# Two buffers of their own for the second token block's adding DMAs, and fourteen row block pairs at other places, in a two-layer decoder trunk

## The chip, the core and the metric

The kernel runs on one core of a Trainium2 chip. The metric is the time of one execution on the device in microseconds (us); where several executions are told, it is their median. A profiled execution gives a trace, and its span runs from the first to the last instruction of the program.

## The reference, cut to what matters

256 tokens of 2048 values pass two layers. Each layer has a token mixer (forgetting attention, then dilated attention) and an MLP, and everything is added into one residual stream `x`:

```
def sq_relu_mlp(h, w_up, w_down):
    a = jax.nn.relu(h @ w_up)          # 2048 -> 8192
    return (a * a) @ w_down            # 8192 -> 2048
...
for i in range(DEPTH):                 # 2 layers
    h = rms_norm(x, mix_norm_g[i])
    mix = fox_attention(...) if i % 2 == 0 else dilated_attention(...)
    x = x + mix
    h = rms_norm(x, mlp_norm_g[i])
    x = x + sq_relu_mlp(h, mlp_w_up[i], mlp_w_down[i])
```

All is float32. The change touches the two MLPs alone; in names, `n1` is the first layer's MLP and `n3` the second's.

## The kernel before

**Matrix products.** The tokens are two blocks of 128, `t=0` and `t=1`. A weight is loaded in raw row blocks of 256 rows by 512 columns (`raw`, five buffers, loaded from SyncE's queue, called SP). ACT copies such a block to a rounded high part (`wh`, line 370), DVE subtracts to get the low part (`wl`, line 371), five buffers each, and TensorE (PE) multiplies three times: high by high, high by low, low by high (lines 421 to 423). That is one *product unit*: 12 matmuls of 512 columns. By how much `wl` is done ahead of its use is called the lead here; ACT can run ahead of PE by the five buffers.

**The MLP.** Its 8192 hidden columns are four blocks, b = 0 to 3. For each block the up projection gives four chunks of 512 columns, which are squared and turned (lines 965 to 1013), and the down projection, `out_proj`, adds the block's part to `x` in four column chunks, n = 0 to 3. For blocks 1 to 3 the up projection's chunks 0 to 2 are computed in another way: a row block pair is cut in halves, and a 2 by 2 block product is done with seven products in place of eight (`SEVEN`, `slice_steps`). One such *pair* (the change's "row block pairs in halves") is one raw load, sums of weight quarters on DVE (`quarters`, lines 380 to 384), two casts and two subtractions (lines 366 to 371, shapes 128x768 and 128x1024), and 21 matmuls (lines 1056 to 1060, output `halves`). These pairs do not stand in a row: they are woven between the product units of the down projection of the block before. The tables `BETWEEN` and `FIRST_BETWEEN` (for b = 1) say after which product unit, counted from the start of that down projection, each of the 24 pairs of a block stands. Units 0 to 15 are chunks n = 0 and 1 in two parts, 16 to 23 are n = 2, 24 to 31 are n = 3, and 32 to 39 are the next block's up projection chunk 3.

**The adding DMAs.** For blocks 0 to 2 the sums of a down projection are not added by DVE but by DMA (`late` in `add_chain`): ACT scales half a chunk of one token block from PSUM into a buffer `y`, and a DMA from GpSimd's queue (POOL) adds it to `x`. A chunk has four y's, two for each token block. There are 4 chunks, 3 blocks and 2 MLPs, so 24 such places and 96 y's.

**What sets the order.** The code is one long program of generators that a counter of steps drives (`Jobs`, `tick`, one step per half product unit; `yield 4` waits four steps, and `clear(steps)` waits so that it wakes on the step without a cast). Each engine executes in exactly the order in which the program issued its instructions (`pin`). An instruction that waits therefore holds everything behind it on its engine. `split` issues the cast and subtraction of the unit five ahead, and issues the next raw load.

Of the kernel before, what the change touches and what calls it, by code (L numbers as in the profile page):

```python
# [9 lines left out]
F32 = mybir.dt.float32  # L10
# [7 lines left out]
P = 128  # L18
# [24 lines left out]
HC = NC // 2  # L43
# [2 lines left out]
SEVEN = ((0, 0, 2, 5), (1, 0, 0, 4), (2, 0, 1, 0), (3, 0, 7, 6), (0, 1, 5, 3), (1, 1, 6, 2), (2, 1, 4, 1))  # L46
SUM_TAGS = ("kh3", "kl3", "kh4", "kl4", "kh5", "kl5", "q0", "q1", "q2", "qkw0", "qkw1", "qkw2", "vh", "vl", "pT", "t1")

BETWEEN = (0, 1, 2, 3, 6, 7, 9, 11, 14, 15, 16, 17, 19, 20, 22, 23, 27, 28, 30, 32, 33, 34, 36, 37)
FIRST_BETWEEN = (0, 1, 2, 5, 7, 9, 10, 11, 15, 16, 17, 18, 20, 21, 22, 23, 27, 28, 30, 31, 33, 34, 36, 37)  # L50


class Jobs:
# [48 lines left out]
def trunk(ctx: ExitStack, tc, x, fox_w_in, fox_b_f, fox_q_gain, fox_k_gain, fox_w_out, dil_w_in,  # L102
# [5 lines left out]
    def clear(steps):  # L108

        return steps + (jobs.now + steps + 1) % 2  # L110
# [21 lines left out]
    work = ctx.enter_context(tc.tile_pool(name="work", bufs=1))  # L132
# [147 lines left out]
    def in_halves():  # L280

        for b in range(1, 4):
            for i, at in enumerate(BETWEEN if b > 1 else FIRST_BETWEEN):
                yield 40 * b - 8 + at, b, i // 8, i % 8
# [115 lines left out]
    def by_column(acc, apart=NC // 2):  # L400
        return acc.rearrange("p (b n h) -> p b h n", n=apart, h=2)

    def halves(t, apart=NC // 2):
        return t.rearrange("p (b h n) -> p b h n", n=apart, h=2)

    used = [0]
# [512 lines left out]
    def add_chain(acc, n, then, ready, scale, late):  # L919
        yield scale and (scale, "rstd") or 0  # L920
        for t in range(NT):
            at = halves(xt[n][:, t, :])
            if late:

                for h in range(2):
                    y = work.tile([P, HC], F32, tag="bias", name=f"y_{scale}_{n}_{t}_{h}_{used[0]}", bufs=2)
                    nc.scalar.activation(y, by_column(acc[t])[:, 0, h, :], AF.Copy, scale=rstd[scale, 2][:, t:t + 1])
                    nc.gpsimd.dma_start(xt[n][:, t, h * HC:h * HC + HC], y, accum_op=ALU.add)  # L928
                if t == 0:
                    yield clear(3)  # L930
                continue
            if scale:
                nc.vector.scalar_tensor_tensor(at, by_column(acc[t]), rstd[scale, 2][:, t:t + 1], at, ALU.mult, ALU.add)
            else:
                nc.vector.tensor_add(at, at, by_column(acc[t]))
            if ready is not None:
                ready(n, t)
        if then is not None:
            jobs.spawn(then(n))
        yield 0  # L940
# [10 lines left out]
    def out_proj(keys, lhs, then=None, ready=None, scale=None, group=0, parts=OUT_PARTS, late=False):  # L951
        posts = [lambda acc, n=n: add_chain(acc, n, then, ready, scale, late) for n in range(NX)]
        if group:
            in_group(lambda n: sums(*(() if n < 2 else (ps_sc, "sc") if scale else (ps_tp, "tp"))),
                     lambda acc, ks: product_steps(acc, keys, lhs, ks), posts[0:group], parts)
        for n in range(group, NX):
            if ready is not None and n == NX - 1:
                last_product(keys, lhs, final_add(n, scale))
            else:
                product(keys, lhs, posts[n])  # L960
# [200 lines left out]
    tag = "n0"  # L1161
# [56 lines left out]
```

## Time and profile before

| | |
|---|---|
| median of 3 runs | 2160.63 us (2159.32 to 2161.76) |
| the profiled execution's own time | 2162.61 us |
| its span | 2160.9 us |
| mean granted TensorE clock | 0.997 |
| PE busy | 2123.3 us (98%) |
| DVE busy | 1748.1 us (81%) |
| ACT busy | 1282.3 us (59%) |
| POOL busy | 138.9 us (6%) |

The first MLP's y's are written between 502.7 and 934.5 us, the second's between 1614.9 and 2050.1 us. An operand of matmul rows reads `out<-in`: `acc` is a product unit's PSUM sum, `halves` that of a pair. In a row of waits, the numbers are microseconds in total, how many times, and the longest. A matmul's duration overlaps the next one's, so pace is read from starts.

### The profile page before, as it was taken

Reading aid. Unit: us, or ns where it says so; the run is one execution under the profiler, and the core shown is the slowest. Engines: PE = TensorE matmul, PEld = TensorE weight load, DVE = VectorE, ACT = ScalarE, POOL = GpSimd, SP = SyncE. Lnnn points to the kernel's source line nnn. Section 1 sums busy time; section 2 is a strip of 40 time slices with the busy share of each in tenths; the row PEclk is TensorE's granted clock in tenths of the full one; section 3 lists DMA queues with packets and bytes.
Section 4 is the critical chain, followed back from the end, with each engine's and each line's share of the span. In section 5 each row is a group of like instructions: output and inputs, shape, how many; then the busy total and the mean of one; then the engine's idle time right before and its main releaser. Section 6 shows DMA issues by size and latency. Waiting matters only on the chain.

```text
span 2160.9 us, 32247 instructions
## 1 busy us (share of the span) xinstructions
PE 2123.3 (98%) x11375; PEld 1889.1 (87%) x11375; DVE 1748.1 (81%) x2548; ACT 1282.3 (59%) x1869; POOL 138.9 (6%) x160
## 2 busy tenths in 40 slices
PE   9999999999999999999999999999999999999999
PEld 7888888898888899898888888888898888888988
DVE  6888876798888898888668787767898798898874
ACT  6565655655665566565655565646655665665662
POOL 2000000001001100100010010000001101101100
PEclk9999999999999999999999999999999999999999
DMA  7888777877777777888877777868868777877784
GB/s 250 260 259 270 250 243 244 275 223 235 233 215 233 233 230 248 234 259 265 266 235 234 240 235 217 264 199 271 262 218 238 214 248 229 238 238 225 239 263 161
DMA packets 374993, 518.26 MB, mean 240 GB/s; under 512 B 43096, under 2 KB 176560, under 8 KB 374832
## 3 DMA queue, kind: packets, MB, share of 16 engines
q1 hardware_dynamic: 360592, 503.23, 73.3%
q0 software_dynamic: 13824, 12.59, 3.9%
q8 instruction: 89, 1.46, 0.3%
q14 instruction: 72, 0.59, 0.1%
q10 hardware_dynamic: 416, 0.39, 0.1%
HBM read 463.12 MB, written 40.39 MB: 233 GB/s over the span
## 4 chain that ended last, share of the span: by engine, by line
PE 64%; issue 12%; DVE 11%; DMA 6%; ACT 4%; POOL 1%; SPq 1%; ACTq 0%; DVEq 0%; POOLq 0%
PE acc L422 19%; PE acc L423 19%; PE acc L421 19%; DVE wl L371 5%; DMA x<-y_n 4%; ACT wh L370 3%; PE halves_n L1059 2%; PE halves_n L1060 2%; PE halves_n L1058 2%; DVE quarters L380 1%; POOL x L928 1%; DVE quarters L383 1%; DVE quarters L384 1%; DMA raw<-in_dil_w_in_dram 1%; DMA raw<-in_mlp_w_down_dram 1%
## 5 line engine op out<-in xcount | busy, mean ns | idle before, releaser
L371 DVE TENSOR_TENSOR wl<-raw,wh 128x1024 fp32r<-128x1024 f32 (+1 forms) x659 | 789.2, 1213 | 303.0 <-ACT wh L370 298.0
L370 ACT CAST wh<-raw 128x1024 fp32r<-128x1024 f32 (+1 forms) x659 | 677.4, 1043 | 402.5 <-PE acc L423 312.1
L421 PE MATMUL acc<-wh,hT_n 128*128 128x512 f32 x1344 | 513.0, 382 | 0.3 <-ACT hT_n L566 0.3
L422 PE MATMUL acc<-wl,hT_n 128*128 128x512 f32 x1344 | 509.7, 379 | 0.9 <-DVE wl L371 0.9
L423 PE MATMUL acc<-wh,hT_n 128*128 128x512 f32 x1344 | 509.5, 379 | 0.0
L370 ACT CAST wh<-quarters 128x1024 fp32r<-128x1024 f32 x144 | 150.7, 1046 | 267.4 <-DVE quarters L384 236.4
L423 PEld LDWEIGHTS acc<-wh,hT_n 128*128 128x128 f32 x1344 | 254.0, 189 | 36.2 <-DVE hT_n L567 0.2
L422 PEld LDWEIGHTS acc<-wl,hT_n 128*128 128x128 f32 x1344 | 254.4, 189 | 35.2 <-DVE wl L371 1.8
L421 PEld LDWEIGHTS acc<-wh,hT_n 128*128 128x128 f32 x1344 | 254.4, 189 | 34.5 <-ACT hT_n L566 0.6
L371 DVE TENSOR_TENSOR wl<-quarters,wh 128x1024 fp32r<-128x1024 f32 x144 | 175.9, 1222 | 50.4 <-ACT wh L370 50.4
L422 PE MATMUL acc<-wl,aTh_n1a 128*128 128x512 f32 x512 | 195.9, 383 | 3.4 <-DVE wl L371 3.1
L421 PE MATMUL acc<-wh,aTh_n1a 128*128 128x512 f32 x512 | 195.1, 381 | 2.9 <-ACT wh L370 2.8
L423 PE MATMUL acc<-wh,aTl_n1a 128*128 128x512 f32 x512 | 194.7, 380 | 0.0
L421 PE MATMUL acc<-wh,aTh_n3a 128*128 128x512 f32 x480 | 183.5, 382 | 4.1 <-ACT wh L370 3.9
L422 PE MATMUL acc<-wl,aTh_n3a 128*128 128x512 f32 x480 | 183.9, 383 | 3.3 <-DVE wl L371 3.1
L423 PE MATMUL acc<-wh,aTl_n3a 128*128 128x512 f32 x480 | 182.9, 381 | 0.0
L1060 PE MATMUL halves_n<-wh,sums_n 128*128 128x256 f32 x576 | 158.8, 276 | 0.0
L1059 PE MATMUL halves_n<-wl,sums_n 128*128 128x256 f32 x576 | 158.8, 276 | 0.0
L1058 PE MATMUL halves_n<-wh,sums_n 128*128 128x256 f32 x558 | 153.9, 276 | 0.0
L368 DVE TENSOR_TENSOR wl<-raw,wh 128x768 fp32r<-128x768 f32 x144 | 137.0, 952 | 2.0 <-ACT wh L366 2.0
L1059 PE MATMUL halves_n<-wl,hT_n 128*128 128x256 f32 x432 | 123.6, 286 | 12.9 <-DVE wl L371 10.8
L366 ACT CAST wh<-raw 128x768 fp32r<-128x768 f32 x144 | 119.7, 831 | 19.0 <-DMA raw<-in_mlp_w_up_dram 7.9
(664 smaller groups left out, 3381.4 us busy)
## 6 DMA issues: line engine op xcount, KB each, us to landing
raw<-in_mlp_w_up_dram SPq DMA_DIRECT2D x256, 512.0 KB, 4.8
raw<-in_mlp_w_down_dram SPq DMA_DIRECT2D x256, 512.0 KB, 4.8
raw<-in_dil_w_in_dram SPq DMA_DIRECT2D x192, 256.0 KB, 3.5
raw<-in_fox_w_in_dram SPq DMA_DIRECT2D x95, 512.0 KB, 4.9
raw<-in_fox_w_out_dram SPq DMA_DIRECT2D x32, 512.0 KB, 4.6
raw<-in_dil_w_in_dram SPq DMA_DIRECT2D x32, 512.0 KB, 4.6
raw<-in_dil_w_out_dram SPq DMA_DIRECT2D x32, 512.0 KB, 4.1
x<-y_n POOLq DMA_DIRECT2D x96, 128.0 KB, 5.0
```

The costliest lines, as they stand in the source:

```text
L366: nc.scalar.copy(flat_hi, flat)
L368: nc.vector.tensor_sub(flat_lo, flat, flat_hi.bitcast(F32))
L370: nc.scalar.copy(hi[:, part, :], raw[:, part, :])
L371: nc.vector.tensor_sub(lo[:, part, :], raw[:, part, :], hi[:, part, :].bitcast(F32))
L380: nc.vector.tensor_sub(t[:, 0, :].rearrange("p (q n) -> p q n", q=2), raw.rearrange("p k n -> p (k n)")[:, HC:3 * HC].rearrange("p (q n) - ...
L383: nc.vector.tensor_add(c, raw[:, 0, HC:NC], neg)
L421: nc.tensor.matmul(acc[t], ah[:, tok], hi, start=first, stop=False)
L422: nc.tensor.matmul(acc[t], ah[:, tok], lo, start=False, stop=False)
L423: nc.tensor.matmul(acc[t], al[:, tok], hi, start=False, stop=last)
L1058: nc.tensor.matmul(to, ah, hi, start=pr == 0 and i == 3, stop=False)
L1059: nc.tensor.matmul(to, ah, lo, start=False, stop=False)
L1060: nc.tensor.matmul(to, al, hi, start=False, stop=pr == KC // 2 - 1 and i > 2)
```

## The change

The y's of t=1 no longer share the two `bias` buffers with those of t=0. They take one buffer each under the tags `t0` and `t2`, which hold a mask and the distance tables of the attention stages and nothing in the MLPs. They are issued two steps earlier (`clear(1)` for `clear(3)`). In the tables, three of the 24 pairs of block 1 stand one product unit later; of blocks 2 and 3, one pair stands one unit later and one a unit earlier. With two MLPs that is 6 + 4 pairs later and 4 earlier.

```
-BETWEEN = (0, 1, 2, 3, 6, 7, 9, 11, 14, 15, 16, 17, 19, 20, 22, 23, 27, 28, 30, 32, 33, 34, 36, 37)
-FIRST_BETWEEN = (0, 1, 2, 5, 7, 9, 10, 11, 15, 16, 17, 18, 20, 21, 22, 23, 27, 28, 30, 31, 33, 34, 36, 37)
+BETWEEN = (0, 1, 2, 3, 6, 7, 9, 11, 14, 15, 16, 17, 19, 21, 22, 23, 27, 28, 30, 31, 33, 34, 36, 37)
+FIRST_BETWEEN = (0, 1, 2, 6, 8, 9, 10, 11, 15, 16, 17, 19, 20, 21, 22, 23, 27, 28, 30, 31, 33, 34, 36, 37)
...
                 for h in range(2):
-                    y = work.tile([P, HC], F32, tag="bias", name=f"y_{scale}_{n}_{t}_{h}_{used[0]}", bufs=2)
+                    of, bufs = ("bias", 2) if t == 0 else (("t0", "t2")[h], 1)
+                    y = work.tile([P, HC], F32, tag=of, name=f"y_{scale}_{n}_{t}_{h}_{used[0]}", bufs=bufs)
                     nc.scalar.activation(y, by_column(acc[t])[:, 0, h, :], AF.Copy, scale=rstd[scale, 2][:, t:t + 1])
                     nc.gpsimd.dma_start(xt[n][:, t, h * HC:h * HC + HC], y, accum_op=ALU.add)
                 if t == 0:
-                    yield clear(3)
+                    yield clear(1)
                 continue
```

The added line shifts the numbers of all later lines by one.

First place: ACT in the first MLP, at the end of column chunk 1 of the second block's down projection. Names are `y_n1_<chunk>_<t>_<half>_...`. Before:

```order
L366 CAST wh288_7145<-raw253_6986 128x768
L927 ACTIVATE y_n1_1_0_0_284_7153<-acc260_0_6665,rstd2_n1_4065 128x256
L927 ACTIVATE y_n1_1_0_1_284_7156<-acc260_0_6665,rstd2_n1_4065 128x256
L370 CAST wh289_7174<-quarters253_7148 128x1024
L370 CAST wh290_7189<-raw254_7038 128x1024
L927 ACTIVATE y_n1_1_1_0_286_7195<-acc260_1_6666,rstd2_n1_4065 128x256
L927 ACTIVATE y_n1_1_1_1_286_7198<-acc260_1_6666,rstd2_n1_4065 128x256
L370 CAST wh291_7213<-raw255_7065 128x1024
```

The same place on ACT after the change:

```order
L366 CAST wh288_7145<-raw253_6992 128x768
L928 ACTIVATE y_n1_1_0_0_284_7153<-acc260_0_6665,rstd2_n1_4065 128x256
L928 ACTIVATE y_n1_1_0_1_284_7156<-acc260_0_6665,rstd2_n1_4065 128x256
L928 ACTIVATE y_n1_1_1_0_284_7168<-acc260_1_6666,rstd2_n1_4065 128x256
L928 ACTIVATE y_n1_1_1_1_284_7171<-acc260_1_6666,rstd2_n1_4065 128x256
L370 CAST wh289_7180<-quarters253_7148 128x1024
L370 CAST wh290_7195<-raw254_7038 128x1024
L370 CAST wh291_7213<-raw255_7065 128x1024
```

The two y's of t=1 moved ahead of two casts, right behind those of t=0.

Second place: ACT in the first MLP, at the end of chunk 3 of the second block's down projection, where a pair moved from unit 32 to 31. Before:

```order
L366 CAST wh322_7820<-raw278_7716 128x768
L927 ACTIVATE y_n1_3_0_0_318_7828<-acc304_0_7532,rstd2_n1_4065 128x256
L927 ACTIVATE y_n1_3_0_1_318_7831<-acc304_0_7532,rstd2_n1_4065 128x256
L1008 CAST aTh_n1a2_0_7842<-turned_n1a2_0_0_7040 128x4x128
L1008 CAST aTh_n1a2_1_7845<-turned_n1a2_1_0_7607 128x4x128
L370 CAST wh323_7854<-quarters278_7823 128x1024
L370 CAST wh324_7871<-raw279_7735 128x1024
L1008 CAST aTh_n1a2_0_7842<-turned_n1a2_0_1_7091 128x4x128
L1008 CAST aTh_n1a2_1_7845<-turned_n1a2_1_1_7637 128x4x128
L927 ACTIVATE y_n1_3_1_0_320_7879<-acc304_1_7533,rstd2_n1_4065 128x256
L927 ACTIVATE y_n1_3_1_1_320_7882<-acc304_1_7533,rstd2_n1_4065 128x256
```

The same place on ACT after the change:

```order
L366 CAST wh322_7820<-raw278_7716 128x768
L370 CAST wh323_7837<-quarters278_7823 128x1024
L370 CAST wh324_7855<-raw279_7735 128x1024
L928 ACTIVATE y_n1_3_0_0_320_7861<-acc304_0_7532,rstd2_n1_4065 128x256
L928 ACTIVATE y_n1_3_0_1_320_7864<-acc304_0_7532,rstd2_n1_4065 128x256
L1009 CAST aTh_n1a2_0_7875<-turned_n1a2_0_0_7040 128x4x128
L1009 CAST aTh_n1a2_1_7878<-turned_n1a2_1_0_7607 128x4x128
L928 ACTIVATE y_n1_3_1_0_320_7881<-acc304_1_7533,rstd2_n1_4065 128x256
L928 ACTIVATE y_n1_3_1_1_320_7884<-acc304_1_7533,rstd2_n1_4065 128x256
```

The pair's matmuls now come before the y's of this chunk, so two casts stand ahead of the y's that stood behind them.

Third place: ACT in the first MLP, in block 1's first pairs (`FIRST_BETWEEN`, 5 to 6 and 7 to 8). Before:

```order
L370 CAST wh171_4763<-raw168_4632 128x1024
L366 CAST wh172_4778<-raw169_4659 128x768
L544 CAST sums_n1_6_0_4786<-room_n1_4076 128x512
L370 CAST wh173_4801<-quarters169_4781 128x1024
L370 CAST wh174_4820<-raw170_4709 128x1024
L1008 CAST aTh_n1a0_3_4834<-turned_n1a0_3_0_4635 128x4x128
```

The same place on ACT after the change:

```order
L370 CAST wh171_4763<-raw168_4632 128x1024
L370 CAST wh172_4778<-raw169_4659 128x1024
L544 CAST sums_n1_6_0_4784<-room_n1_4076 128x512
L366 CAST wh173_4799<-raw170_4709 128x768
L370 CAST wh174_4820<-quarters170_4802 128x1024
L1009 CAST aTh_n1a0_3_4834<-turned_n1a0_3_0_4635 128x4x128
```

The cast of a whole raw block (128x1024, from `raw`), which stood fifth, is now second, and the pair's two casts follow it.

## The prediction, as it was put on record

> **What bounds the kernel now.** I read the page first, then the waits of TensorE, then the tile `y_n` (the scaled sums that the adding DMAs take), then busy time by stage. The page says that TensorE is the bound, with little left over:
>
> ```profile
> span 2160.9 us, 32247 instructions
> PE 2123.3 (98%) x11375; PEld 1889.1 (87%) x11375; DVE 1748.1 (81%) x2548; ACT 1282.3 (59%) x1869; POOL 138.9 (6%) x160
> ```
>
> TensorE idles 2160.9 - 2123.3 = 37.6 us. From 500 to 2054 us, where both MLPs lie, it waits for the high and low weight parts that ACT (`wh`) and DVE (`wl`) make:
>
> ```profile
> PE halves_n L1059 <- DVE wl L371: 10.8, 21, 0.9
> PE acc L422 <- DVE wl L371: 6.8, 10, 0.8
> PE acc L421 <- ACT wh L370: 6.7, 5, 2.2
> PE halves_n L1058 <- ACT wh L370: 3.1, 2, 2.1
> ```
>
> The tile `y_n` tells what holds ACT. In its view the second part is what ACT, the writer, waited for ahead of these instructions:
>
> ```profile
> L927 ACT ACTIVATE y_n<-acc,rstd_n x96: 457/474/483, 502.7 to 2050.1; 128x256 f32<-128x256 f32 x96
> ...
> its engine sat idle before it (us, times) until:
> ...
>   DMA x<-y_n: 89.2, 45
> ...
> DMA to landing us min/median/max: 2.6/5.0/8.7
> ```
>
> 96 y's are written at 24 places (a column chunk n of a down projection), four each. The two of the second token block (t=1) reuse the buffers of the two of t=0, so ACT stands until those DMAs land: 45 of 48 times, 89.2 us. Everything behind them in ACT's queue, casts above all, stands too. One place, by the timelines of TensorE, ACT and DVE:
>
> ```profile
> 705.45 0.48 PE L421 MATMUL acc<-wh,aTh_n1a 128*128 128x512 f32 x1 [1.88 <-ACT wh L370]
> 706.71 0.80 PE L422 MATMUL acc<-wl,aTh_n1a 128*128 128x512 f32 x1 [0.78 <-DVE wl L371]
> ...
> 701.88 0.47 ACT L927 ACTIVATE y_n<-acc,rstd_n 128x256 f32<-128x256 f32 x1 [2.75 <-DMA x<-y_n]
> 703.99 0.47 ACT L927 ACTIVATE y_n<-acc,rstd_n 128x256 f32<-128x256 f32 x1 [1.64 <-DMA x<-y_n]
> ...
> 705.43 1.23 DVE L371 TENSOR_TENSOR wl<-raw,wh 128x1024 fp32r<-128x1024 f32 x1 [4.86 <-ACT wh L370]
> ```
>
> ACT stands 2.75 + 1.64 us, DVE therefore idles 4.86 us, and TensorE, whose lead is used up, 1.88 + 0.78 us. I cut the MLPs into stretches with y's (POOL busy over 11 us) and without:
>
> ```profile
> 500.00:610.00 110.00, 103.08 (x606) 91.78 (x605) 91.17 (x126) 64.74 (x93) 14.68 (x18) 1.00 0.78 229
> 610.00:684.00 74.00, 72.21 (x431) 65.30 (x430) 67.44 (x95) 44.41 (x60) 2.94 (x5) 1.00 0.75 238
> 684.00:770.00 86.00, 83.25 (x501) 75.36 (x500) 71.89 (x99) 54.14 (x78) 11.79 (x15) 0.98 0.81 233
> 770.00:850.00 80.00, 79.18 (x474) 71.76 (x473) 74.06 (x101) 48.76 (x64) 2.47 (x5) 1.00 0.78 246
> 850.00:940.00 90.00, 87.73 (x535) 79.35 (x534) 77.25 (x108) 57.82 (x83) 13.02 (x17) 1.00 0.83 234
> 1612.00:1720.00 108.00, 101.41 (x595) 91.09 (x594) 89.55 (x125) 63.32 (x92) 14.40 (x18) 0.98 0.79 229
> 1720.00:1790.00 70.00, 69.44 (x419) 63.12 (x418) 64.45 (x86) 44.30 (x60) 0.79 (x3) 1.00 0.75 245
> 1790.00:1882.00 92.00, 87.98 (x529) 79.36 (x528) 77.06 (x110) 56.50 (x82) 13.88 (x17) 1.00 0.80 231
> 1882.00:1960.00 78.00, 76.38 (x459) 69.06 (x459) 70.86 (x95) 47.01 (x63) 0.63 (x3) 1.00 0.75 242
> 1960.00:2054.00 94.00, 91.08 (x537) 82.23 (x536) 78.73 (x112) 58.35 (x84) 14.01 (x17) 0.96 0.80 229
> ```
>
> Columns: stretch, length, busy PE, PEld, DVE, ACT, POOL, granted clock, DMA share, GB/s. Length minus PE busy is TensorE's idle time: with y's 6.92 + 2.75 + 2.27 + 6.59 + 4.02 + 2.92 = 25.47 us, without 1.79 + 0.82 + 0.56 + 1.62 = 4.79 us. Three stretches have a clock under 1.00:
>
> ```profile
> 706.63:710.05 3.42, 3.34 (x8) 0.50 0.62 180
> 1713.57:1716.98 3.41, 2.99 (x13) 0.50 0.26 38
> 1812.55:1815.96 3.41, 1.71 (x9) 1.00 1.08 369
> 1986.63:1993.46 6.83, 6.29 (x16) 0.50 0.74 199
> ```
>
> (PE alone, then clock, DMA share, GB/s.) At 706.63, inside the second stall above, the clock halves for 3.42 us; twice more it halves, and each time a stall of about 2 us (2.2 and 2.1 are the longest in the table of waits) has just ended. The stretch from 1812.55, busy for 1.71 of 3.41 us, keeps it. Work at half clock loses half of its time: (3.34 + 2.99 + 6.29) / 2 = 6.31 us that stand as "busy".
>
> **The change, part by part.** (1) *Own buffers for t=1.* Its y's go to `t0` and `t2`, whose last user is the place before; between the two closest places TensorE has four product units and two pairs, 15 us by the times in (4), and the slowest DMA landed in 8.7 us, so no y waits any longer. 89.2 us of ACT waiting go. TensorE's share of that is at most the 25.47 us of its stretches, at least the first stalls of each place, 6.7 + 3.1 + 6.8 = 16.6 us. The `L1059` waits, 10.8 us, come while DVE makes up for what it lost; they go if it then has a lead. DVE was busy 91.17 of 110 us in the first stretch, and TensorE needs 103: with the waits gone DVE has the time. I take 25.47 - 2 left over.
>
> (2) *Two steps earlier.* The y's of t=1 now stand right behind those of t=0, which puts 2 x 0.47 us of ACT ahead of the next cast. What hides it: ACT is busy 64.74 of 110 us. Without that cover it costs 24 x 0.95 = 23 us; I take nothing. On POOL the same four DMAs a place are issued in one go; its only other work there are fills of a weight buffer, and POOL is busy 14.68 of 110 us. SP gets no new instruction and no new wait.
>
> (3) *Half clock.* If the stalls of about 2 us go, 6.31 us go with them; bounds 0 and 6.31, and I take 6.31, as the stalls named are the y's.
>
> (4) *The moved pairs.* A pair is a raw load, two casts, five DVE operations and 21 matmuls, and all of it moves by one product unit (12 matmuls). Its price is the lead, from DVE's and TensorE's starts:
>
> ```profile
> 706.58 0.69 DVE L380 TENSOR_TENSOR quarters<-raw 128x512 f32<-128x512 f32 x1
> ...
> 710.49 1.22 DVE L371 TENSOR_TENSOR wl<-raw,wh 128x1024 fp32r<-128x1024 f32 x1
> 711.62 0.69 DVE L380 TENSOR_TENSOR quarters<-raw 128x512 f32<-128x512 f32 x1
> ...
> 693.74 0.28 PE L1058 MATMUL halves_n<-wh,sums_n 128*128 128x256 f32 x1
> 693.85 0.28 PE L1059 MATMUL halves_n<-wl,sums_n 128*128 128x256 f32 x1
> ...
> 702.76 0.38 PE L421 MATMUL acc<-wh,aTh_n1a 128*128 128x512 f32 x1
> 702.98 0.38 PE L422 MATMUL acc<-wl,aTh_n1a 128*128 128x512 f32 x1
> ```
>
> DVE takes 710.49 - 706.58 = 3.9 us for a pair, TensorE 21 x 0.11 = 2.3; a product unit is 1.1 against 12 x 0.22 = 2.6. So a pair costs 1.6 us of lead and a unit gives back 1.5. In both MLPs three pairs of the first block and one of each later block come a unit later (10): they meet 1.5 us more lead. One of each later block comes a unit earlier (4), just ahead of the y's of n=3: at most 4 x 1.5 = 6 us. Neither kind stands at a stall now (the first block's early places, and the first of the four):
>
> ```profile
> 450.00:500.00 50.00, 50.00 (x311) 46.01 (x310) 47.87 (x72) 29.79 (x37) 0.00 (x0) 1.00 0.67 209
> 760.00:776.00 16.00, 15.99 (x105) 14.73 (x104) 15.22 (x22) 10.57 (x16) 3.49 (x4) 1.00 0.86 223
> ```
>
> I take +1, between 0 and 6. Of the 4.79 us away from the y's, which a carried lead may shorten, I take 2 off (bounds 0 and 4.79).
>
> Sum: 2160.9 - 25.47 + 2 - 6.31 + 1 - 2 = 2130.1 us of span. The profiled execution took 2162.61 us, 1.7 more than its span, and lies 2.0 above the median of the runs, 2160.63; I leave both in, as they cancel, and forecast **2130 us**, 1.4% faster. The floor, with every MLP stall gone, is 2160.9 - 30.26 - 6.31 = 2124.3.
>
> [...]
> [...]
>
> **The rivals.** A, *DVE takes over as the bound*: ACT is free, but DVE, busy 91 to 93% in the stretches without y's (74.06 of 80), never builds the lead, and the 10.8 us of `L1059` and the 4.79 elsewhere stay. Only 16.6 and 6.31 go: 2160.9 - 22.9 = 2138. For it speaks that stretch, against it the 4.86 us of DVE idleness that each long wait causes.
> B, *the clock halves anyway*: 2130 + 6.31 = 2136. Against it, all three times follow a long stall.
> C, *the moved pairs or late loads eat part*: 6 us at the early pairs and half of the 25.47 kept: 2148.
> D, *slower: four adding DMAs at once make the weight loads late.* Loads take longer where y's are in flight; in the first row of 694 to 706 us, in the second of 708 to 720 us, without any:
>
> ```profile
> raw<-in_mlp_w_down_dram SPq DMA_DIRECT2D x2, 512.0 KB, 6.4
> ...
> raw<-in_mlp_w_down_dram SPq DMA_DIRECT2D x3, 512.0 KB, 3.8
> ```
>
> Two y's in flight cost 2.6 us; four might cost 5.2, landing in 9. Five raw buffers cover about four product units, 10 us. It decides from there: each microsecond beyond costs 24 us over the places, so landings of 12 us would cost 48 and end near 2178.
> E, *nothing happens*: the y's of t=1 wait in another way (for the place before), and the 24 places stay: 2160.
>
> **How the numbers follow.** A measurement of this kernel tells 0.2%, 4.3 us, from no change. Chances: forecast 0.62 (own range 2125 to 2135), A 0.18, B 0.07, C 0.07, D 0.03, E 0.03. The range of 8 in 10 starts at the floor, 2124, and takes in A and B: up to 2144. Faster is all but D and E: 0.94; same 0.03; slower 0.03.
>
> **What the profile after would show.** No ACT wait for `DMA x<-y_n`, or a few microseconds. TensorE's waits on `wh` at `L421` and `L1058` gone, on `wl` under 8 us in all. PE busy near 2117, and no stretch of clock 0.50 between 500 and 2054. y's landing a little later than 5.0 us. Wrong I would be if ACT's waits went and TensorE's `L1059` waits grew (A), if half-clock stretches stayed without long stalls (B), if waits for raw loads grew (D), or if TensorE stalled before the y's of n=3 (C).

## The result, and the profile after

The changed kernel takes 2112.69 us (2111.84 to 2114.57, 5 runs), the kernel before on the same chip 2161.76 us (2159.32 to 2166.59, 5 runs): a ratio of 0.9772, with an interval from 0.9757 to 0.9786. It is 2.3% faster, where 1.4% was forecast. The time lies under the whole range (2124 to 2144 us) and 12 us under what the prediction called the floor. The profiled execution took 2114.57 us, with a span of 2112.7 us.

The first lines of the page of the kernel after:

```profile
span 2112.7 us, 32198 instructions
...
PE 2101.5 (99%) x11375; PEld 1881.5 (89%) x11375; DVE 1747.3 (83%) x2548; ACT 1287.3 (61%) x1869; POOL 139.9 (7%) x160
```

The span fell by 48.2 us and the busy time of TensorE (PE) by 21.8 us, for the same 11375 matmuls. The idle time, span minus busy, fell only from 37.6 to 11.2 us. So nearly half of the gain was never listed as idle time. The change did what it says. In the view of the tile `y_n` the wait for `DMA x<-y_n`, 89.2 us before, is not there:

```profile
L928 ACT ACTIVATE y_n<-acc,rstd_n x96: 457/477/496, 502.3 to 1998.7; 128x256 f32<-128x256 f32 x96
...
its engine sat idle before it (us, times) until:
  ACT y_n L928: 230.0, 23
...
DMA to landing us min/median/max: 3.2/6.9/10.1
```

(The 230.0 us are POOL's, which waits for the y's and has nothing else to do; one line number is added by the change.) TensorE's waits between 500 and 2054 us, where the four longest of before came to 27.4 us (10.8 + 6.8 + 6.7 + 3.1), are down to three groups:

```profile
PE halves_n L1060 <- DVE wl L368: 2.3, 4, 0.8
PE halves_n L1060 <- DVE wl L371: 1.1, 4, 0.3
PE po_d L681 <- DVE pT_d L710: 1.0, 1, 1.0
```

Busy time by stage, first both MLPs of the kernel before (`500.00:940.00`, `1612.00:2054.00`), then stretches of the kernel after that hold the same work within a few matmuls: the first one with y's, the first one without, and both MLPs. The columns are those of the prediction's stretches, with the number of matmuls behind PE.

```profile
500.00:940.00 440.00, 425.44 (x2539) 383.56 (x2538) 381.81 (x525) 269.86 (x376) 44.89 (x58) 1.00 0.79 235
1612.00:2054.00 442.00, 426.29 (x2532) 384.87 (x2531) 380.65 (x525) 269.48 (x375) 43.72 (x56) 0.99 0.78 234
```

```profile
500.00:599.00 99.00, 99.00 (x604) 90.80 (x603) 92.40 (x129) 65.45 (x93) 14.88 (x18) 1.00 0.87 257
599.00:672.00 73.00, 72.11 (x434) 65.66 (x434) 65.51 (x92) 46.42 (x64) 4.14 (x6) 1.00 0.77 237
...
500.00:917.00 417.00, 415.66 (x2537) 380.89 (x2536) 382.71 (x527) 271.82 (x376) 45.37 (x58) 1.00 0.83 249
1589.00:2006.00 417.00, 414.95 (x2530) 380.19 (x2529) 382.00 (x526) 271.16 (x376) 44.22 (x56) 1.00 0.84 249
```

The two MLPs take 834 us in place of 882, so the whole gain is there. Look at the first stretch: 606 matmuls took 110 us before, of which 6.92 us were listed as idle, and 604 take 99 us now. At least 10.6 us went where the profile showed 6.92, and the granted clock was 1.00 in both stretches.

### The profile page after: what moved, and what is told of

Its sections match the earlier page's. It is cut to its first block, busy times and chain, and to the rows that moved or that the text cites. A ratio compares the mean times of both kernels' runs of the same rounds, so it can differ in the third digit from the quotient of the medians.

```text
span 2112.7 us, 32198 instructions
## 1 busy us (share of the span) xinstructions
PE 2101.5 (99%) x11375; PEld 1881.5 (89%) x11375; DVE 1747.3 (83%) x2548; ACT 1287.3 (61%) x1869; POOL 139.9 (7%) x160
## 4 chain that ended last, share of the span: by engine, by line
PE 91%; DVE 4%; DMA 2%; ACT 1%; issue 1%; SPq 1%; ACTq 0%; DVEq 0%
PE acc L421 25%; PE acc L422 25%; PE acc L423 25%; PE halves_n L1060 5%; PE halves_n L1061 5%; PE halves_n L1059 5%; DVE wl L371 2%; ACT wh L370 1%; PE halves_n L1057 0%; DMA raw<-in_dil_w_in_dram 0%; DMA turned_n1a<-blocks_n1a 0%; PE sc_d L733 0%; SPq L317 0%; DMA raw<-in_fox_w_in_dram 0%; DVE quarters L380 0%
```

## Experiments

**Which part of the change does it.** The change has three parts: own buffers for the y's of the second token block, these y's two steps earlier, and the two tables of pairs. Three kernels take them apart; a fourth, made later, has the early place alone. The first has the tables alone (lines of the changed kernel with `-`, of the experiment with `+`):

```
-  of, bufs = ("bias", 2) if t == 0 else (("t0", "t2")[h], 1)
-  y = work.tile([P, HC], F32, tag=of, ..., bufs=bufs)
+  y = work.tile([P, HC], F32, tag="bias", ..., bufs=2)
...
-  yield clear(1)
+  yield clear(3)
```

> Only the two tables of the change; the y's of t=1 still share buffers with those of t=0. Theory L (all of the gain is ACT no longer standing for the y's DMAs): about 2161 us like before, within 5; ACT's waits for the y DMAs stay near 89 us. Rival T (the 12 us below my floor came from the moved pairs): 2145 to 2150 us.

The second has own buffers alone: the old `BETWEEN` and `FIRST_BETWEEN`, and the old place:

```
-  yield clear(1)
+  yield clear(3)
```

> Only the two buffers of their own; the y's of t=1 stay three to four steps behind, the tables are the old ones. L: 2113 to 2120 us, ACT's waits for the y DMAs near 0, TensorE's listed idle time falls by some 25 us and the time by some 45. T: 2125 to 2132 us, my forecast without the 12 us. Rival E (the two steps earlier matter, since they free the sums' banks earlier): 2130 us or more.

The third has own buffers and the early place, with the old tables (the changed kernel with `BETWEEN` and `FIRST_BETWEEN` of the kernel before):

> Own buffers and two steps earlier, with the old tables. L: like the run with buffers alone within 3 us, and 0 to 4 us above the whole change. T: 12 us or more above the whole change. E: equal to the whole change, and well below buffers alone.

Measured: tables alone 2178.12 us, 1.0082 of the kernel before (1.0066 to 1.0097); own buffers alone 2112.44 us, 0.9776 (0.9761 to 0.9791); own buffers and early place 2113.50 us, 0.9780 (0.9764 to 0.9797). Own buffers alone are the whole change within what the runs can tell, and the other two parts add nothing to them. Without them the new tables cost 0.8%. The waits of ACT (tile `y_n`) and of TensorE with the tables alone:

```profile
  DMA x<-y_n: 94.6, 47
```

```profile
PE halves_n L1059 <- DVE wl L371: 12.4, 22, 0.9
PE halves_n L1058 <- ACT wh L370: 8.1, 6, 2.0
PE acc L421 <- ACT wh L370: 7.9, 5, 2.2
PE acc L422 <- DVE wl L371: 6.3, 10, 0.8
```

ACT stood only 5.4 us longer than in the kernel before, and TensorE waited longer for `wh`. Some 8 of the 16 us are half clock: the trace has 30.7 us at a clock of 0.50 (mean clock 0.993), where that of the kernel before has 13.7 (0.997), and half of TensorE's busy time in them is 14.4 us against 6.3. That the moved pairs took lead where it was needed is the likely reason for the longer waits, but no run shows the lead itself. The fourth kernel is the kernel before with the early place alone:

```
 t=1, kernel before with one edit:
-  yield clear(3)
+  yield clear(1)
```

> The kernel before with one edit: the y's of the second token block two steps earlier, right behind those of the first, in the buffers shared with them and with the old tables. Theory L (ACT's standing is what costs): ACT reaches them earlier, after the same landing, so it stands longer, by up to the time of the two steps, some 1 to 2 us at a place: slower than before, 2165 to 2210 us. A rival (the place alone is worth something, for the y's land earlier and the next block starts earlier): as before or faster, 2140 to 2162 us.

Measured: 2237.11 us, 1.0347 (1.033 to 1.0365), beyond what either theory gave. The tile `y_n`, then TensorE:

```profile
  DMA x<-y_n: 147.2, 48
```

```profile
PE halves_n L1058 <- ACT wh L370: 29.9, 10, 5.5
PE halves_n L1056 <- DVE c_n3a L1028: 17.5, 6, 4.7
PE halves_n L1056 <- DVE c_n1a L1028: 15.5, 6, 4.1
```

ACT reaches the y's of the second block earlier, meets the same transfers and stands 147.2 us. Then a second kind of wait comes in: TensorE finds the banks of its `halves` still unread, because DVE's sums of them (`c_n1a`, `c_n3a`) are late too. So the early place is free only with own buffers.

**How much ACT's standing costs.** If that is the whole cause, holding ACT by its own work must bring the time back, with no DMA involved. The first such kernel is the whole change with a long hold:

```
-  nc.scalar.activation(y, by_column(acc[t])[:, 0, h, :], ...)
+  for _ in range(11 if t and h else 1):
+      nc.scalar.activation(y, by_column(acc[t])[:, 0, h, :], ...)
```

> The whole change, but the last y of each of the 24 places is computed eleven times instead of once (same value), which holds ACT about 10 x 0.36 = 3.6 us at each place, near the mean of 89.2 / 24 = 3.7 us that it stood there before. L: most of the gain is lost, 2140 to 2160 us, and the clock may halve again. Rival (the own buffers help by the DMAs or PSUM, not by ACT's time): 2113 to 2118 us.

The second has the same hold, but the old tables and the old place, that is own buffers alone and the hold:

> Own buffers, with the old tables of pairs and the y's of the second token block three steps after those of the first, as the kernel before has them; only the last of the four y's at each place is computed eleven times over by ACT (the output stays what it was). So no DMA holds ACT, but ACT's own work does, for 10 x 0.36 = 3.6 us a place, near the 89.2 / 24 = 3.7 us that it stood in the kernel before. Theory L (ACT's time away from the casts is what costs, whatever takes it): near the kernel before, 2150 to 2172 us. A rival (the DMAs themselves, serialised by the shared buffers, cost the time, for instance by making the weight loads late): no more than 2125 us. The same hold with the new tables and the early place made 2201.7 us; L lays the difference to the tables and the place, as with the shared buffers, where the new tables alone cost 16 us.

The third is the whole change with `range(5 ...)` in place of 11:

> The changed kernel, but the last of the four y's at each place is computed five times over by ACT (the output stays what it was), so ACT is held for 4 x 0.36 = 1.4 us more at each of the 24 places, where the long hold (ten times over, 3.6 us) made 2201.7 us. Theory L (what counts is the lead of the weight parts over TensorE, 3.5 to 6 us at these places in the changed kernel, 0 to 1.5 us in the one before): 1.4 us is covered by the lead and costs next to nothing, 2113 to 2122 us. Theory P (each microsecond of ACT's standing costs TensorE a fixed share, whatever the lead): by the long hold, (2201.7 - 2112.7) / (24 x 3.6 us) = 1.03 us for each, so 24 x 1.4 x 1.03 = 35 us, near 2147.

The holds were longer than the 0.36 us a repeat that the expectations took, as the timelines of ACT show for the four y's of a place (first the kernel after, then the hold of 5):

```profile
714.43 1.57 ACT L928 ACTIVATE y_n<-acc,rstd_n 128x256 f32<-128x256 f32 x4
```

```profile
667.34 3.60 ACT L929 ACTIVATE y_n<-acc,rstd_n 128x256 f32<-128x256 f32 x8
```

Four repeats take 3.60 - 1.57 = 2.03 us, 0.51 each; the ten repeats took 5.09 us in the same way (fourteen in 6.66 us), and 5.06 us with the old tables. Measured: long hold 2201.66 us, 1.0188 (1.0173 to 1.0203); long hold with old tables and place 2195.90 us, 1.0167 (1.0149 to 1.0184); short hold 2124.71 us, 0.9841 (0.9827 to 0.9856). The longest waits of TensorE with the long hold at the old place, and with the short hold:

```profile
PE halves_n L1061 <- DVE wl L371: 15.4, 25, 1.1
PE acc L421 <- ACT wh L370: 9.4, 4, 2.4
PE halves_n L1060 <- ACT wh L366: 8.2, 6, 2.1
PE halves_n L1060 <- ACT wh L370: 5.3, 2, 2.7
```

```profile
PE halves_n L1061 <- DVE wl L371: 4.6, 12, 0.6
PE halves_n L1058 <- DVE c_n3a L1030: 2.6, 2, 1.3
PE halves_n L1058 <- DVE c_n1a L1030: 2.6, 2, 1.3
PE halves_n L1061 <- DVE wl L368: 2.4, 4, 0.8
```

The long hold brings back waits like those of the kernel before (`wh` up to 2.1 to 2.7 us, against 2.1 and 2.2, and `wl` behind it), and no transfer holds ACT there: the view of `y_n` lists no wait for a DMA. That refutes the rival that the DMAs themselves cost the time, which allowed 2125 us at most. With the short hold, 5.2 us of TensorE's waits are of the second kind seen above, for sums of `halves` on DVE (`c_n1a`, `c_n3a`); DVE itself stands there for a cast of ACT (2.29 us at 671.91), with these sums behind it in its queue. The ranges that my theory gave were wrong each time, though: 2140 to 2160 us expected and 2201.7 measured, 2150 to 2172 expected and 2195.9 measured, 2113 to 2122 expected and 2124.7 measured (theory P, at 2147, lay further off). And the long hold costs about the same with the new tables and the early place as with the old ones (the intervals overlap), so laying the difference to the tables was wrong too. What the cost goes by, in the main, is the size of each hold. Set in order, with the cost over the changed kernel as ratio minus 0.9773, times 2161 us, and with half of TensorE's busy time at a clock of 0.50 as the part that is half clock:

| kernel | ACT held, us | cost, us | of it half clock, us | cost per us |
|---|---|---|---|---|
| short hold | 24 x 2.03 = 49 | 14.7 | 0 | 0.30 |
| kernel before | 89.2 (DMA) | 49 | 6 | 0.55 |
| tables alone | 94.6 (DMA) | 67 | 14 | 0.71 |
| long hold, old place | 24 x 5.06 = 121 | 85 | 23 | 0.70 |
| long hold, whole change | 24 x 5.09 = 122 | 90 | 26 | 0.73 |
| early place alone | 147.2 (DMA) | 124 | 28 | 0.84 |

Between the short hold and the long hold at the old place a microsecond costs (85 - 14.7) / (121 - 49) = 0.97 us, and (85 - 23 - 14.7) / (121 - 49) = 0.66 us without the half clock. Drawn back to no cost, that leaves some 49 - 14.7 / 0.97 = 34 us free, 1.4 us a place, or 27 us and 1.1 without the half clock. This is an estimate from two kernels that also differ in tables and place: 1.1 to 1.4 us of standing is swallowed at each place, and what is beyond costs about its full length, a third of it through the clock. The line through these two gives 54, 59 and 110 us for the three DMA holds, where 49, 67 and 124 were measured; so they lie near it, not on it.

**Why the profile listed less than was lost.** The next experiment cuts nothing but the lead, at all places alike:

```
-W_BUFS = 5
+W_BUFS = 4
```

> The changed kernel with four instead of five buffers for each weight part (wh, wl), so that the casts can run less far ahead of TensorE, at all places alike. Many short waits are expected rather than a few long ones. Theory O (a matmul's record of 0.38 us reaches 0.16 us past the start of the next one, so the first 0.16 us of every stall stands as busy time and shorter stalls stand as no idle time at all): the span rises by clearly more than the listed idle time of TensorE does, 1.5 to 3 times as much (it was 48.2 to 26.4 us from the kernel before to the changed one). A rival (the additional time came from TensorE itself working slower in the kernel before, by its clock or by contention in its memory): the span rises as much as the idle time, within 10%, since nothing but the buffers differs. As to the size: 2120 to 2190 us, a guess.

Measured: 2147.43 us (2144.63 to 2148.05), 0.9947 of the kernel before (0.9931 to 0.9964). The mean clock was 1.000. The page, and TensorE's waits from 500 to 2054 us:

```profile
span 2142.9 us, 32182 instructions
...
PE 2113.8 (99%) x11375; PEld 1883.3 (88%) x11375; DVE 1750.6 (82%) x2548; ACT 1288.5 (60%) x1869; POOL 139.9 (7%) x160
```

```profile
PE halves_n L1060 <- DVE wl L371: 9.8, 19, 1.1
PE halves_n L1060 <- DVE wl L368: 9.2, 11, 0.9
PE acc L422 <- DVE wl L371: 0.8, 2, 0.5
```

Against the kernel after, the span rose by 30.2 us and span minus busy by 29.1 - 11.2 = 17.9 us: 1.69 times as much, inside the 1.5 to 3 of theory O and far from the rival's "within 10%". The other 12.3 us stand as busy time of the same 11375 matmuls, at a clock of 1.000. Two places in the timeline of the kernel before show how. The columns are start, length, and the listed idle time in brackets:

```profile
521.52 0.38 PE L421 MATMUL acc<-wh,aTh_n1a 128*128 128x512 f32 x1
521.98 0.48 PE L422 MATMUL acc<-wl,aTh_n1a 128*128 128x512 f32 x1
522.30 0.38 PE L423 MATMUL acc<-wh,aTl_n1a 128*128 128x512 f32 x1
522.52 0.38 PE L421 MATMUL acc<-wh,aTh_n1a 128*128 128x512 f32 x1
...
568.44 0.48 PE L421 MATMUL acc<-wh,aTh_n1a 128*128 128x512 f32 x1
569.70 0.48 PE L422 MATMUL acc<-wl,aTh_n1a 128*128 128x512 f32 x1 [0.78 <-DVE wl L371]
570.02 0.38 PE L423 MATMUL acc<-wh,aTl_n1a 128*128 128x512 f32 x1
```

The matmul of 128x512 at 522.30 stands with 0.38 us, but the next starts 522.52 - 522.30 = 0.22 us later, so 0.16 us of its record lie over its successor. At 521.52 the next start comes 0.46 us later, 0.24 too late, and no wait is listed. The matmul behind it, at 521.98, stands with 0.48 us, and its successor starts 0.32 us later, another 0.10 us. So 0.34 us were lost and no wait is listed (0.08 us of it is idle time, too short for a bracket). At 568.44 the lost time is 1.26 - 0.22 + 0.10 = 1.14 us, of which 0.78 are listed.

For the whole trace I took, from the starts of all matmuls, the time from each start to the next over the pace of its shape (0.216 us for 128x512 and 0.111 for 128x256, as most starts stand apart in the traces before and after), in us, with the number of starts:

| starts | before | after | four buffers |
|---|---|---|---|
| behind a listed wait over 0.15 us | 40.6 (46) | 8.2 (13) | 30.5 (41) |
| behind idle time up to 0.15 us, which gets no bracket | 3.9 (17) | 0 | 0.5 (1) |
| 0.06 to 0.13 us late, nothing listed | 16.0 (173) | 9.8 (113) | 15.5 (168) |
| later still, nothing listed (before, most of it half clock) | 7.9 | 2.4 | 3.4 |
| all others | 4.1 | 3.9 | 4.6 |
| sum | 72.5 | 24.3 | 54.5 |

The sums differ by 48.2 and 30.2 us, as the spans do. This is arithmetic on the trace and not a model.

**A better version.** The waits for `wl` left in the MLPs of the kernel after, 3.4 us in all, stand at the start of later blocks (645, 807, 1734 and 1897 us, two at each), right behind two pairs that the change had not moved. The edit moves them one product unit on:

```
-BETWEEN = (0, 1, 2, 3, 6, 7, 9, 11, ...)
+BETWEEN = (0, 1, 2, 4, 6, 8, 9, 11, ...)
```

> The changed kernel, with the two pairs that come fourth and sixth in each later block one product unit later, since its four longest stalls inside the MLPs (at 645, 807, 1734 and 1897 us, 0.45 to 1.03 us each, 3.4 us listed) stand right behind these pairs at the blocks' starts. If a unit gives back 1.5 us of lead, as forecast, all four go, with 0.16 us more that stands as busy for each stall: 2108 to 2111 us. If the stalls only move to another place: 2112 to 2115 us.

Measured: 2109.55 us (2109.14 to 2110.66), 0.9772 (0.9757 to 0.9786), inside the 2108 to 2111 us expected. But the kernel before took 2158.13 us on that chip, so the ratio was the same as the changed kernel's and the comparison showed no gain. Both were run side by side then:

> The changed kernel once more, beside its variant with two pairs later on the same chip, since 4 us are to be told apart and the kernel before differs by about that from chip to chip. All theories: 2109 to 2115 us, 0.976 to 0.9785 of the kernel before.

> The variant with the fourth and sixth pair of each later block one product unit later, beside the changed kernel on the same chip. If the pairs' place has a price of its own also where ACT is free: 3 to 4 us (0.14 to 0.18%) under the changed kernel, as the spans of the two profiled executions were (2108.9 and 2112.7 us). If the first comparison, where both stood at 0.9772 of the kernel before, was right: no difference.

Measured: changed kernel 2112.78 us (2112.76 to 2113.16), 0.9773 (0.9758 to 0.9788); two pairs later 2109.31 us (2108.82 to 2110.30), 0.9757 (0.9743 to 0.9772). Side by side the ranges of the runs lie 2.5 us apart, and the medians 3.5 us. It beats both kernels, by 0.16% (2109.31 / 2112.78) and 2.4%. Not all the waits went: at 1887 and 1889 us TensorE now waits where it did not before, 1.7 us in place of 3.4. What it still waits for apart from the start, above all:

```profile
PE halves_n L1060 <- DVE wl L371: 1.1, 1, 1.1
PE halves_n L1060 <- DVE wl L368: 0.6, 1, 0.6
...
PE po_d L681 <- DVE pT_d L710: 0.5, 1, 0.5
```

## Why the prediction was right in direction and wrong in size

**The step that failed** is "Length minus PE busy is TensorE's idle time", and with it the terms 25.47 and 4.79 us, the floor of 2124.3 us that was to bound the range, and "PE busy near 2117" (it is 2101.5). In the listed measure the change took 30.27 us of MLP idle time (440 + 442 - 425.44 - 426.29) down to 3.39 (417 + 417 - 415.66 - 414.95), 26.9 us, close to the 25.47 - 2 + 2 that the sum counted. But the waits cost more than is listed: 0.18 to 0.20 us more on average up to the next start (before, 40.6 us were lost behind 46 waits listed with 31.2; after, 8.2 behind 13 with 5.9), and the start behind that was 0.10 us late at 36 of the 46 before. At 568 us it was 0.36 us in all, and at 521 us 0.34 us were lost with no wait listed. Here that made some 16 us: of the 48.2 us, 26.4 were idle time (25.3 in waits over 0.15 us, 1.1 in shorter ones), which leaves 21.8, and of these the half clock is 5.5 by the group of the table that holds most of it, 6.31 as the sum had it. The rest the sum had nowhere. Corrected by this alone it gives about 2114 us. The experiment with four buffers shows the same on a kernel without any half clock. The figure could have been had before: the starts and the pace were in the trace.

**The wait of ACT** went entirely, by the own buffers, as step (1) said. That TensorE's lead covers a part of it was used only through TensorE's own waits; the holds put that part at 1.1 to 1.4 us a place, an estimate.

**Two steps earlier** cost nothing, as step (2) took it: own buffers with and without it stand at 0.9780 and 0.9776. The reason given, ACT's free time, holds only while no transfer is waited for; with shared buffers the same move cost 76 us.

**Half clock.** No stretch under 1.00 is left in the MLPs (1.00 from 500 to 917 and from 1589 to 2006 us), so the 6.31 us went, as step (3) took it, and rival B, that the clock halves anyway, fell. That work loses half of its time there shows in the starts: in the half-clock stretches of the kernel before those of 128x512 stand 0.43 us apart in place of 0.216 (at 708 and 1990 us), those of 128x256 0.21 in place of 0.111 (at 1715 us). The prediction's reading, that a stall of about 2 us brings the half clock, fits the kernel before. These are the 3.41 us ahead of each of the three half-clock stretches in its MLPs (stretch, length, TensorE's busy time, clock, DMA share, GB/s):

```profile
703.22:706.63 3.41, 0.83 (x3) 1.00 1.10 351
1710.16:1713.57 3.41, 0.85 (x6) 1.00 0.52 121
1983.22:1986.63 3.41, 1.26 (x6) 1.00 1.08 381
```

The longest waits that reach into them are of 1.88, 2.10 and 2.22 us. It does not fit the long hold. With the long hold at the old place (mean clock 0.989, 48 us at half clock) this is one of the halvings:

```profile
951.12:954.53 3.41, 1.65 (x10) 1.00 0.64 122
954.53:957.94 3.41, 3.37 (x14) 0.50 0.48 128
```

The waits that reach into the first of the two are of 0.98, 0.62 and 1.07 us. In the kernel before these half-clock stretches start at 706.63, 1713.57 and 1986.63 us, which is 295 and 80 times 3.413 us apart. Cut at that distance from 20 us to the last 4.5 us, its trace has 618 stretches at full clock that no half clock followed; TensorE was busy for 1.71 us in the one from 1812.55 and for 2.04 us or more in all others. So in these rows the half clock went with how little TensorE was busy in such a stretch, and not with the length of one wait. They give no border: 1.65 us at the hold were followed by half clock, 1.71 us in the kernel before were not. With four buffers TensorE had 25 us of listed waits, none over 1.1 us but the one at the start, and the mean clock was 1.000. In the kernel after, cut in the same way, the least busy stretch had 2.37 us.

**The moved pairs** were taken as +1 us, with 6 us as the bound. With own buffers they cost nothing that can be measured (0.9772 against 0.9780 without them). With the shared buffers they cost 16 us, over the bound, some 8 of them through the clock; that the lead that they take was already used up is argued, not shown. That one unit of place is worth something even with ACT free is shown by the better version, though for pairs that the change leaves alone.

**The other rivals.** A (DVE takes over as the bound) fell: DVE is busy 92.40 of 99 us in the first stretch, and the `wl` waits are 3.4 us in all. C and E fell with the time. D, that four adding DMAs at once make the weight loads late, did not come: the landings of the y's went from 5.0 to 6.9 us, at most 10.1, where the prediction had 12 us cost 48, and the loads stayed where they were (4.8 and 4.8 us before):

```profile
raw<-in_mlp_w_up_dram SPq DMA_DIRECT2D x256, 512.0 KB, 4.9
raw<-in_mlp_w_down_dram SPq DMA_DIRECT2D x256, 512.0 KB, 4.7
...
x<-y_n POOLq DMA_DIRECT2D x96, 128.0 KB, 6.9
```

For the weight loads the trace shows no delay in the median. What makes the landings of the y's longer, no run shows.

What stays open: why the matmul behind a wait takes 0.10 us more, what decides on the clock when TensorE is busy for about half of the 3.41 us (1.65 and 1.71 in the rows above), and how much of the 0.06 to 0.13 us late starts that remain (113 in the kernel after) could be removed.

## What to carry to other kernels

On an engine whose instructions overlap in the records, measure lost time from start to start against the pace of the shape, not as length minus busy: here the second measure missed 45% of what was lost. A shared buffer that makes a producer engine wait for a transfer can cost little up to some length and then about its full length: here 0.30 us for each microsecond that ACT stood with the short hold, and 0.97 for each one more up to the long hold, with the stalls' tails and the half clock counted in. That the lead of the parts it produces covers the first, 1.1 to 1.4 us a place, is an estimate. So give the transfers buffers of their own before anything is moved around them. A move that is free with the wait gone can cost dearly with the wait there (the early place: nothing measurable, and 76 us), so the parts of such a change are to be tried in that order.

## What the runs showed of the hardware that was not expected

In the kernel before, 14 matmuls of 128x512 and 28 of 128x256 at full clock, behind a listed wait over 0.15 us, stand with 0.48 and 0.37 us in place of 0.38 and 0.28; of these, 10 and 26 have no such wait right behind them, and their successors start 0.10 us late (0.32 us later in place of 0.22, 0.21 in place of 0.11). With the holds the same write of ACT, from the same source into the same buffer over and over, starts every 0.51 us; in the kernel after the four y's of a place, in different buffers, start 0.36 us apart ((1.57 - 0.48) / 3, at 714 us). In the kernel before the granted clock fell to 0.50 behind three stretches of 3.41 us in which TensorE was busy for 0.83, 0.85 and 1.26 us, the longest waits there being of 1.88, 2.10 and 2.22 us; with the long hold at the old place also behind one of 1.65 us, with waits of at most 1.07 us. Four adding DMAs of a place land in 6.9 us in the kernel after, in place of 5.0 before, and leave the median of the weight loads where it was (4.9 and 4.7 us against 4.8).
